# Query and key projections in Strassen blocks, in a stage of their own ahead of attention

## The chip, the core and the metric

The kernel runs on one core of a Trainium2 chip. The metric is the device time of one launch in microseconds (us), from the first to the last instruction with what lies around them; lower is better. Before the change it is 963.37 us, the median of 3 runs (961.13 to 970.48). The engines are TensorE (PE in the profile; PEld is its weight load), VectorE (DVE), ScalarE (ACT), GpSimd (POOL) and SyncE (SP), on whose queue every DMA is issued.

## The reference

A decoder block on 1024 rows of 1024 channels: an RMS norm, one wide input projection, two attention branches side by side (FoX with a forgetting bias, and differential attention with rotary embedding), SiLU gates, and a merge by sigmoid gates.

```python
h = rms_norm(x, g_pre[l], NORM_EPS)
proj = jnp.einsum('bsd,dn->bsn', h, w_in[l])
qa, ka, va, fa, za, qb, kb, vb, zb, gates = jnp.split(proj, SPLIT_POINTS, axis=-1)
log_f = jax.nn.log_sigmoid((fa + b_forget[l]).astype(jnp.float32)).transpose(0, 2, 1)
ya = fox_attention(split_heads(qa, FOX_HEADS), split_heads(ka, FOX_HEADS),
                   split_heads(va, FOX_HEADS), log_f)
ya = merge_heads(ya) * jax.nn.silu(za)
qd = apply_rope(qb.reshape(b, s, DIFF_HEADS, 2, DIFF_QK_DIM).transpose(0, 2, 3, 1, 4), cos, sin)
kd = apply_rope(kb.reshape(b, s, DIFF_HEADS, 2, DIFF_QK_DIM).transpose(0, 2, 3, 1, 4), cos, sin)
yb = diff_attention(qd, kd, split_heads(vb, DIFF_HEADS), lam)
yb = rms_norm(yb, g_subln[l], SUBLN_EPS) * (1.0 - lam_init)
yb = merge_heads(yb) * jax.nn.silu(zb)
gate_a, gate_b = jnp.split(jax.nn.sigmoid(gates), N_BRANCHES, axis=-1)
merged = (gate_a * jnp.einsum('bsw,wd->bsd', ya, w_branch[l, 0])
          + gate_b * jnp.einsum('bsw,wd->bsd', yb, w_branch[l, 1]))
x = x + rms_norm(jnp.einsum('bsd,de->bse', merged, w_out[l]), g_post[l], NORM_EPS)
```

## The kernel before, in words

Every product is made from operands split in a high part of fewer mantissa bits and a low part, the rest; a product is then three matmuls: high by high, high by low, low by high. The normed and transposed input `hT` stays on the chip as high and low parts in four blocks each (halves of the channels, `kh`, and of the rows, `sh`).

The work goes through five stages. **Values** (lines 99 to 218): `x_block` norms and transposes 128 rows, `load_wv` loads and splits the value weights for one of 8 channel blocks, and `v_block` makes the values of 128 rows and stores them to DRAM. **Attention** (lines 248 to 612): 8 units, four of the differential branch (diff, u 0 to 3) and then four of the forgetting branch (fox, u 4 to 7, two heads each). For each unit queries and keys are projected (`unit_proj`: two chunks of 512 rows for each, 24 matmuls a chunk, `project`), turned by `rope` in the diff units, and laid by `stack` in four tiles TA, TB, KA, KB. A row block of 128 queries goes through `s_row`: score matmuls (S), a DVE pass that scales, adds the bias or mask and takes the running minimum, the exponential on ACT, a reciprocal on DVE, scaling on POOL. Two row blocks make a group, for which `av` transposes the probabilities on PE (pt), splits them on ACT (ph) and DVE (pl), and multiplies by the values (yp). **Gates** (lines 614 to 810): the merge gates' projection, for one of 8 column blocks in the plain way (`gates_plain`) and for the other 7 by `wino`, which makes a 2 by 2 block product from 7 block products in place of 8 (Winograd's form of Strassen's scheme). Its left operands are sums of weight blocks (S, split into `a`), its right operands blocks of `hT` and four combinations of them, T4 to T7, which `h_combinations` makes at the start of this stage. **Branches** (to line 851), and the **output** product with the last norm, again by `wino`.

The order of the instructions on each engine is set when the program is built, by a scheduler that works from a model of each instruction's duration; each engine then takes its queue in that order. In the attention stage the loop over units lists, beside the groups of unit u, the four projection chunks of unit u+1 and the two chunks of one z projection (`ZFILL`) as fillers between groups; the fillers are PE work that waits for no attention step. Buffers are set by pools: 6 tiles for probabilities (`pp`), 3 score banks (`sps`), 2 banks for transposes.

## Time and profile before

| | |
|---|---|
| runs | 963.37 us median of 3 (961.13 to 970.48) |
| the profiled execution's own time | 964.18 us, span 962.4 us |
| mean granted TensorE clock | 0.981 |
| busy, share of the span | PE 94%, DVE 66%, ACT 45%, POOL 51% |
| values | 0 to 111 us |
| attention with its projections | 111 to 598 us |
| gates | 598 to 773 us |
| branches and output | 773 to 962.4 us |

A row of the profile reads: line, engine, operation, what is written <- what is read, partitions x elements and type, times executed, busy us and mean ns of one, and then the idle time of the engine just before such an instruction, with what ended it. A matmul's recorded duration reaches to the modelled end of its pipeline, so that neighbours overlap; how fast PE goes is read from the count in a stretch. The stage limits in the table are read from the first and last start of pv, pk, pz, pg, x_g and pb matmuls.

### The profile page before, as it was taken

How to read it: one execution, taken by the hardware profiler on the slowest of the kernel's cores; microseconds unless marked ns; L12 is line 12 of the kernel's file. 1: busy time of each engine (PE TensorE's matmuls, PEld its weight loads, DVE VectorE, ACT ScalarE, POOL GpSimd, SP SyncE). 2: the span in 40 equal slices, each digit the busy share in tenths (PEclk: the TensorE clock that was granted, in tenths of full speed). 3: DMA queues.
4: the chain of work that ended last, by engine and by line, in shares of the span. 5: the costliest groups of instructions: out<-in, count | busy, mean ns of one | idle time of the engine just before them, and what ended most of it. 6: DMA issues, size and time to landing. Idle time of an engine off the chain costs nothing.

```text
span 962.4 us, 13682 instructions
## 1 busy us (share of the span) xinstructions
PE 900.5 (94%) x4600; PEld 752.0 (78%) x4600; DVE 635.3 (66%) x1180; ACT 435.9 (45%) x862; POOL 489.6 (51%) x460
## 2 busy tenths in 40 slices
PE   7999989999999999999999998879999989999992
PEld 5999867777887888888888886658887768887871
DVE  7731258978768765656566477985667683559875
ACT  3421125665656674555555566243444361324331
POOL 7100035446545464344533554935566735878972
PEclk9999989999999999999999999989999999999997
DMA  9532444424334341524225231254444697210144
GB/s 315 190 110 93 144 128 112 107 77 120 97 96 137 99 144 43 150 67 130 81 88 146 85 88 56 78 179 149 143 153 134 191 357 247 67 44 1 46 151 153
DMA packets 109896, 120.17 MB, mean 125 GB/s; under 512 B 9969, under 2 KB 79601, under 8 KB 109826
## 3 DMA queue, kind: packets, MB, share of 16 engines
q1 hardware_dynamic: 109826, 119.30, 40.0%
q8 instruction: 36, 0.59, 0.3%
q14 instruction: 34, 0.28, 0.1%
HBM read 77.26 MB, written 29.43 MB: 111 GB/s over the span
## 4 chain that ended last, share of the span: by engine, by line
PE 45%; DVE 17%; POOL 13%; issue 10%; DMA 7%; ACT 6%; SPq 2%; DVEq 0%; POOLq 0%; ACTq 0%
PE pb L835 9%; PE pv L192 9%; PE pz L243 7%; PE pq L243 5%; PE pk L243 4%; POOL S_g L646 3%; PE ypf L444 3%; PE ptf L420 2%; DMA raw<-in_w_in_dram 2%; DMA swk<-rawk 2%; SPq L284 2%; DVE Pd L393 1%; POOL a_g L634 1%; PE ypd L444 1%; PE Sf L391 1%
## 5 line engine op out<-in xcount | busy, mean ns | idle before, releaser
L192 PE MATMUL pv<-wvhi,hT 128*128 128x264 f32 (+2 forms) x384 | 88.8, 323 | 0.4 <-DVE hT L178 0.4
L682 PE MATMUL x_g<-T,a_g 128*128 128x512 f32 x336 | 82.1, 399 | 6.3 <-DVE a_g L634 2.5
L243 PE MATMUL pk<-hT,hi_k 128*128 128x512 f32 x256 | 84.5, 402 | 1.7 <-ACT rawk L280 1.7
L243 PE MATMUL pz<-hT,hi_z 128*128 128x512 f32 x256 | 84.2, 399 | 0.1
L243 PE MATMUL pq<-hT,hi_q 128*128 128x512 f32 x256 | 83.4, 399 | 0.0
L682 PEld LDWEIGHTS x_g<-T,a_g 128*128 128x128 f32 x336 | 63.4, 191 | 23.5 <-DVE a_g L634 4.0
L835 PE MATMUL pb<-yT,hi_br 128*128 128x512 f32 x256 | 78.9, 390 | 1.9 <-ACT hi_br L229 1.6
L682 PE MATMUL x_o<-wo_op,a_o 128*128 128x512 f32 x336 | 77.4, 391 | 2.3 <-ACT a_o L633 1.2
L682 PEld LDWEIGHTS x_o<-wo_op,a_o 128*128 128x128 f32 x336 | 62.8, 188 | 16.9 <-ACT a_o L633 2.1
L192 PEld LDWEIGHTS pv<-wvhi,hT 128*128 128x128 f32 x384 | 64.3, 189 | 6.1 <-DVE hT L178 0.7
L682 PE MATMUL x_g<-hT,a_g 128*128 128x512 f32 x252 | 62.2, 400 | 6.1 <-DVE a_g L634 5.4
L398 ACT ACTIVATE Pd<-Pd,mxd 128x128 f32<-128x128 f32 (+7 forms) x64 | 49.5, 773 | 29.9 <-DVE mxd L393 28.1
L512 POOL TENSOR_SCALAR Pf<-Pf,lf 128x1024 f32<-128x1024 f32 (+3 forms) x64 | 47.9, 752 | 29.0 <-DVE lf L400 27.2
L424 DVE TENSOR_TENSOR plf<-ptf,phf 128x512 fp32r<-128x512 f32 (+1 forms) x80 | 50.0, 635 | 18.8 <-ACT phf L423 17.8
L192 PE MATMUL pv<-wvlo,hT 128*128 128x512 f32 (+2 forms) x192 | 61.8, 324 | 0.6 <-DVE wvlo L148 0.6
L682 PEld LDWEIGHTS x_g<-hT,a_g 128*128 128x128 f32 x252 | 48.4, 193 | 17.6 <-DVE a_g L634 5.8
L482 POOL TENSOR_SCALAR Pd<-Pd,ld 128x128 f32<-128x128 f32 (+7 forms) x32 | 25.5, 798 | 71.1 <-DVE ld L481 38.2
L508 POOL TENSOR_TENSOR cb<-cb,trim 128x128 f32<-128x128 f32 x64 | 29.5, 464 | 63.3 <-DVE mxf L393 46.7
L398 ACT ACTIVATE Pf<-Pf,mxf 128x1024 f32<-128x1024 f32 (+3 forms) x64 | 49.7, 778 | 21.4 <-DVE mxf L393 20.8
L835 PEld LDWEIGHTS pb<-yT,hi_br 128*128 128x128 f32 x256 | 47.8, 188 | 12.7 <-ACT hi_br L229 2.0
L243 PEld LDWEIGHTS pk<-hT,hi_k 128*128 128x128 f32 x256 | 48.0, 192 | 11.2 <-issue 2.1
L243 PEld LDWEIGHTS pq<-hT,hi_q 128*128 128x128 f32 x256 | 48.0, 191 | 9.1
(243 smaller groups left out, 2440.5 us busy)
## 6 DMA issues: line engine op xcount, KB each, us to landing
raw<-in_w_in_dram SPq DMA_DIRECT2D x14, 512.0 KB, 4.0
g_d<-c_g SPq DMA_DIRECT2D x21, 256.0 KB, 2.0
vb_d<-vbs SPq DMA_DIRECT2D x8, 512.0 KB, 5.9
va_d<-vas SPq DMA_DIRECT2D x8, 512.0 KB, 3.0
raw_k<-in_w_in_dram SPq DMA_DIRECT2D x8, 512.0 KB, 4.3
raw_q<-in_w_in_dram SPq DMA_DIRECT2D x8, 512.0 KB, 4.4
V<-vb_d SPq DMA_DIRECT2D x4, 1024.0 KB, 7.4
raw_z<-in_w_in_dram SPq DMA_DIRECT2D x8, 512.0 KB, 5.4
```

The lines of the kernel that those rows point to most:

```text
L192: nc.tensor.matmul(ps[n], lhsT=hT[hp][k // 4][i // 4][:, k % 4, hs], rhs=wt[k][:, a:b], start=first, stop=(k == KT - 1 and hp == 1))
L243: nc.tensor.matmul(ps, lhsT=a[:, k, :], rhs=hT[h][k // 4][c][:, k % 4, :], start=(k == 0 and a is hi and h == 0), stop=(k == KT - 1 and a ...
L284: nc.sync.dma_start(sw[b * 32:(b + 1) * 32, :], raw[o * 32:(o + 1) * 32, :])
L398: nc.scalar.activation(pr[:, 0:n], pr[:, 0:n], AF.Exp, bias=mx[:, len(pcs) - 1:len(pcs)], scale=-1.0, accum_out=le)
L424: nc.vector.tensor_tensor(pl[:, 0:n], pt[:, 0:n], ph[:, 0:n], op=ALU.subtract)
L444: nc.tensor.matmul(o, lhsT=a, rhs=b[:, src], start=(j == 0 and n == 0), stop=(odd == 1 and jj == g and n == len(prods) - 1))
L482: nc.gpsimd.tensor_scalar(p2[:, 0:n], p2[:, 0:n], l2, 1.0, op0=ALU.mult, op1=ALU.mult)
L508: nc.gpsimd.tensor_tensor(diag, diag, trim, op=ALU.add)
L512: nc.gpsimd.tensor_scalar(p1[:, 0:n], p1[:, 0:n], l1, 1.0, op0=ALU.mult, op1=ALU.mult)
L646: eng.tensor_tensor(comb[name], x, y, op=op)
L682: nc.tensor.matmul(x[m], lhsT=a[:, ai, k, :], rhs=right[m][bi][k], start=(k == 0 and n == 0), stop=(k == 3 and n == 2))
L835: nc.tensor.matmul(ps, lhsT=a[:, kk, :], rhs=yT[g][h][:, k % 2, sl], start=(k == 0 and a is hi and h == 0), stop=(k == 3 and a is lo))
```

## The change

The projections of queries and keys leave the attention loop. Between values and attention stands a new stage: for each of the 8 units the query weights and the key weights are the upper and lower block rows of a left operand, and `wino` makes the queries and keys of both halves of the rows with 7 block products of 12 matmuls. `qk_out` turns the result in the diff units (in place, with the same four small DMAs that exchange halves), splits it into high and low part, and stores both to DRAM (`qk_d`). The units are taken in the order 0, 4, 1, 5, 2, 6, 3, 7. In the attention stage `unit_qk` loads the four tiles with 8 DMAs of 256 KB; `unit_proj`, `rope` and `stack` are gone. The fillers there are the z projections alone, one for each unit (`ZFILL`).

The combinations T4 to T7 are made in the values stage, 16 POOL additions, 16 DVE subtractions, 16 ACT copies and 16 DVE low parts as before, and serve the new stage; they are also stored to DRAM (`t_d`, 8 tiles of 1 MB) and loaded again at the start of the gates. The value weights are loaded and split in two groups, all 8 channel blocks of the diff values and then all 8 of the fox values and the forget column, the second in the first's tiles; all 8 row blocks of the first group come before those of the second.

```diff
-ZFILL = ((0,), (1,), (), (2,), (3,), (4,), (5,), (6, 7))
+ZFILL = ((0,), (1,), (2,), (3,), (4,), (5,), (6,), (7,))
+PAIRS = (0, 4, 1, 5, 2, 6, 3, 7)
+ORD = (1, 6, 5, 7, 2, 3, 4)
...
+    qk_d = [[[dram.tile([P, S], F32, name=f"qk_d{u}_{n}_{part}") for part in range(2)]
+             for n in range(2)] for u in range(8)]
...
+        def load_wv(k, grp):
+            c0, n = ((VB, 512), (VA, 520))[grp]
+            raw = xp.tile([P, 520], F32, tag="wvraw", name=f"wvraw{k}_{grp}", bufs=3)[:, 0:n]
+            nc.sync.dma_start(raw, w[k * P:(k + 1) * P, c0:c0 + n])
+            hi = wv_hi[grp][k] = vw.tile([P, 520], F32R, tag=f"wvhi{k}", name=f"wvhi{k}_{grp}")
+            lo = wv_lo[grp][k] = vw.tile([P, 520], F32R, tag=f"wvlo{k}", name=f"wvlo{k}_{grp}")
...
         for i in range(NB):
             if i + 3 < NB:
                 x_block(i + 3)
-            v_block(i)
+            v_block(i, 0)
+        for k in range(KT):
+            load_wv(k, 1)
+        for i in range(NB):
+            if i < 4:
+                h_combinations(i)
+            v_block(i, 1)
+        for m, ts in t_tiles.items():
+            for part in range(2):
+                nc.sync.dma_start(t_d[m][part], f32(ts[part]))
...
+        def qk_out(u, n, c, t):
+            sl = slice(c * CH, (c + 1) * CH)
+            nm = f"{u}_{n}_{c}"
+            if u < 4:
+                sw = rp.tile([P, CH], F32, tag="sw", name=f"sw{nm}")
+                for b in range(4):
+                    o = b ^ 1
+                    nc.sync.dma_start(sw[b * 32:(b + 1) * 32, :], t[o * 32:(o + 1) * 32, :])
+                nc.vector.tensor_tensor(t, t, cosT[:, sl], op=ALU.mult)
+                nc.gpsimd.tensor_tensor(sw, sw, sinT[:, sl], op=ALU.mult)
+                nc.vector.tensor_tensor(t, t, sw, op=ALU.add)
+            hi = rp.tile([P, CH], F32R, tag="qh", name=f"qh{nm}")
+            lo = rp.tile([P, CH], F32R, tag="ql", name=f"ql{nm}")
+            nc.scalar.copy(hi, t)
+            nc.vector.tensor_tensor(lo, t, hi, op=ALU.subtract)
+            for part, p in enumerate((hi, lo)):
+                nc.sync.dma_start(qk_d[u][n][part][:, sl], f32(p))
+
+        for u in PAIRS:
+            c0 = (QB, KB_) if u < 4 else (QA, KA_)
+            raw = []
+            for n in range(2):
+                r = wpool.tile([P, KT, P], F32, tag="wraw", name=f"rawqk{u}_{n}")
+                nc.sync.dma_start(r, w_cols(c0[n] + u % 4 * P))
+                raw.append(r)
+            left = left_operands(f"p{u}", raw[0][:, 0:4], raw[0][:, 4:8], raw[1][:, 0:4], raw[1][:, 4:8])
+            run_all(wino(f"p{u}", left, h_ops, ORD,
+                         *(lambda t, u=u, n=n, c=c: qk_out(u, n, c, t)
+                           for n in range(2) for c in range(2))))
...
-        def unit_proj(u):
...
+        def unit_qk(u):
+
+            T = {}
+            for m, h in enumerate("AB"):
+                for n, nm in enumerate("KT"):
+                    t = T[nm + h] = qk.tile([P, S], F32R, tag=nm + h, name=f"{nm}{h}{u}")
+                    for part, rows in enumerate((UPR, DNR)):
+                        nc.sync.dma_start(
+                            f32(t[rows]), qk_d[u][1 - n][part][m * 64:(m + 1) * 64])
+            return T
...
-    h_combinations()
+    for m in (6, 5, 7, 4):
+        ts = [tpool.tile([P, 4, CH], F32R, tag=f"T{m}{part}", name=f"U{m}{part}")
+              for part in range(2)]
+        for part in range(2):
+            nc.sync.dma_start(f32(ts[part]), t_d[m][part])
+        h_ops[m] = [[t[:, k, :] for k in range(4)] for t in ts]
     gates_plain(0)
```

How the order moves is shown at two places. The first is VectorE in the values stage, and before the change the start of the gates. Before, after the last attention step (`ys` is the sum of a fox group's two halves), the combinations stand one behind the other: `f` are the full blocks that are subtracted in place, `T` the low parts of the combinations.

```order
L776 TENSOR_TENSOR f_0_6759<-f_0_6757,f_0_6759 128x512
L780 TENSOR_TENSOR f_0_6757<-f_0_6761,f_0_6757 128x512
L773 TENSOR_TENSOR T_6750<-f_0_6759,T_6749 128x512
L773 TENSOR_TENSOR T_6754<-f_0_6757,T_6753 128x512
L778 TENSOR_TENSOR f_0_6759<-f_0_6761,f_0_6759 128x512
L782 TENSOR_TENSOR f_0_6763<-f_0_6763,f_0_6759 128x512
L776 TENSOR_TENSOR f_1_6779<-f_1_6777,f_1_6779 128x512
```

After the change the same steps stand in the values stage where the second group of weights comes in: `wvlo_1` are the low parts of that group's weights, for which PE waits, and `vas` is the first evacuation of a result of that group.

```order
L278 TENSOR_TENSOR wvlo_1_704<-wvraw_1_701,wvhi_1_703 128x520
L363 TENSOR_TENSOR f_1_807<-f_1_807,f_1_806 128x512
L278 TENSOR_TENSOR wvlo_1_710<-wvraw_1_707,wvhi_1_709 128x520
L353 TENSOR_TENSOR T_179<-f_1_806,T_178 128x512
...
L278 TENSOR_TENSOR wvlo_1_722<-wvraw_1_719,wvhi_1_721 128x520
L357 TENSOR_TENSOR f_2_881<-f_2_881 128x512
L361 TENSOR_TENSOR f_2_881<-f_2_882,f_2_881 128x512
L353 TENSOR_TENSOR T_177<-f_2_881,T_176 128x512
L278 TENSOR_TENSOR wvlo_1_728<-wvraw_1_725,wvhi_1_727 128x520
L359 TENSOR_TENSOR f_2_881<-f_2_882,f_2_881 128x512
L353 TENSOR_TENSOR T_181<-f_2_881,T_180 128x512
L337 TENSOR_TENSOR vas_799<-pv_10_749,vas_799 128x4x64
```

The weights' low parts, the evacuation and the combinations now share VectorE's queue; from the first combination to this evacuation it holds 12 of the 16 steps `f`, 10 of the 16 steps `T` and all 8 steps `wvlo_1`.

The second place is TensorE inside a fox unit, between the last groups of one unit and the first of the next. Before, projection chunks of the unit after (`pk`, `pq`) stand between the attention steps.

```order
L243 MATMUL pk_1_5521<-hT_91,hi_k_5364 128x512
L243 MATMUL pk_1_5521<-hT_95,hi_k_5364 128x512
L444 MATMUL ypf_0_1_5171<-phf_0_1_0_5173,V_4550 128x256
L444 MATMUL ypf_0_1_5171<-plf_0_1_0_5174,V_4550 128x256
...
L420 MATMUL ptf_1_1_1_5240<-ident,Pf_1_2_5161 128x128
...
L391 MATMUL Sf_0_6_0_5333<-KA_4558,TA_4556 128x512
L392 MATMUL Sf_0_6_0_5333<-KA_4558,X0f_3_5313 128x512
L243 MATMUL pk_1_5521<-hT_91,lo_k_5365 128x512
...
L243 MATMUL pq_1_5550<-hT_89,hi_q_5399 128x512
```

After the change attention steps stand there alone.

```order
L527 MATMUL Sf_1_6_0_5451<-KB_5306,X1f_3_5431 128x512
L579 MATMUL ypf_0_0_5283<-phf_0_0_0_5285,V_4634 128x256
L579 MATMUL ypf_0_0_5283<-plf_0_0_0_5286,V_4634 128x256
...
L526 MATMUL Sf_1_6_1_5455<-KB_5306,TB_5309 128x384
...
L526 MATMUL Sf_0_5_0_5537<-KA_5300,TA_5303 128x512
...
L526 MATMUL Sf_0_4_1_5556<-KA_5300,TA_5303 128x256
L527 MATMUL Sf_0_4_1_5556<-KA_5300,X0f_2_5532 128x256
L555 MATMUL ptf_0_3_0_5464<-ident,Pf_0_6_5337 128x128
```

The fillers that are left, the z chunks, are not spread evenly either: the scheduler puts the z projections 0 to 3 into unit 0, one into the start of each of units 2, 3 and 4, the last into the middle of unit 4, and none into units 1, 5, 6 and 7.

397 lines of the change are left out of this document (179 added, 218 removed).

## The prediction

> **What bounds the kernel now.** I read the head of the page first, then the shares of the chain that ended last, then busy time by stage, then the groups.
>
> ```profile
> span 962.4 us, 13682 instructions
> PE 900.5 (94%) x4600; PEld 752.0 (78%) x4600; DVE 635.3 (66%) x1180; ACT 435.9 (45%) x862; POOL 489.6 (51%) x460
> PE 45%; DVE 17%; POOL 13%; issue 10%; DMA 7%; ACT 6%; SPq 2%; DVEq 0%; POOLq 0%; ACTq 0%
> ```
>
> TensorE is busy for 94% of the span, yet it holds only 45% of the chain, and DVE and POOL hold 30%. So PE's work bounds the kernel in some stretches and the handing on between the engines in others. The windows (start:end, length, busy us and instructions of PE, PEld, DVE, ACT, POOL, then granted PE clock, DMA share, GB/s) show which.
>
> ```profile
> 0.00:111.00 111.00, 104.30 (x646) 91.98 (x647) 48.31 (x80) 29.95 (x61) 26.72 (x48) 1.00 0.49 171
> 111.00:598.00 487.00, 468.41 (x2552) 395.67 (x2550) 333.67 (x834) 277.08 (x586) 225.42 (x250) 0.99 0.36 102
> 165.00:185.00 20.00, 17.87 (x84) 14.51 (x83) 19.64 (x37) 10.18 (x21) 10.40 (x8) 0.91 0.45 112
> 565.00:598.00 33.00, 29.30 (x201) 24.58 (x199) 25.92 (x80) 26.07 (x60) 17.80 (x29) 1.00 0.15 45
> 598.00:640.00 42.00, 33.32 (x127) 26.00 (x127) 38.19 (x32) 13.95 (x25) 32.27 (x21) 0.88 0.27 88
> 640.00:773.00 133.00, 128.75 (x558) 103.67 (x557) 88.25 (x105) 55.94 (x96) 79.70 (x54) 1.00 0.54 172
> 680.00:700.00 20.00, 20.00 (x90) 16.56 (x89) 11.90 (x16) 7.83 (x15) 11.39 (x9) 1.00 0.52 158
> 773.00:962.00 189.00, 165.72 (x723) 134.64 (x721) 126.88 (x131) 59.00 (x98) 125.48 (x89) 0.97 0.39 131
> ```
>
> Values (first row) and the later gates (640 to 773) are PE's. At 680 to 700, 90 matmuls of 128x512 fill 20 us: **0.222 us each**, the price used below (0.433 ns a column). The start of the gates (598 to 640) is DVE's: 38.2 of 42 us busy, and PE has only 127 matmuls, 28 us of work. Attention is mixed: at 165 to 185 DVE is busy 98% of the time, while over the whole stage it is 69%.
>
> **Arithmetic.** Queries and keys take 8 x 4 chunks x 24 = 768 matmuls before and 8 x 7 x 12 = 672 after. 96 x 0.222 = 21.3 us is all that PE saves. What decides is how well each new stage is filled.
>
> **Attention without its fillers.** What a unit asks of PE and of DVE comes from these rows (fox first, then diff; each covers 4 units).
>
> ```profile
> 567.62 1.04 PE L420 MATMUL ptf<-ident,Pf 128*128 128x128 f32 x8
> 568.41 0.36 PE L391 MATMUL Sf<-KA,TA 128*128 128x256 f32 x1
> L420 PE MATMUL ptf<-ident,Pf 128*128 128x128 f32 x288 | 44.2, 275 | 2.0 <-DVE plf L424 1.9
> L444 PE MATMUL ypf<-phf,V 128*128 128x256 f32 (+1 forms) x160 | 42.2, 285 | 1.0 <-DVE ys L522 0.4 <-ACT phf L423 0.3
> L391 PE MATMUL Sf<-KA,TA 128*128 128x512 f32 (+3 forms) x48 | 17.5, 366 | 0.6 <-DVE mxf L393 0.6
> L243 PE MATMUL pz<-hT,lo_z x128: 387/389/628, 172.1 to 565.7; 128*128 128x512 f32 x128
> L424 DVE TENSOR_TENSOR plf<-ptf,phf 128x512 fp32r<-128x512 f32 (+1 forms) x80 | 50.0, 635 | 18.8 <-ACT phf L423 17.8
> L393 DVE CUSTOM_DVE_ANT_0 Pf<-Sf,cb 128x512 f32<-128x512 f32 (+1 forms) x64 | 36.4, 569 | 22.0 <-PE ptf L420 15.6 <-PE Sf L392 4.7 <-POOL cb L508 0.9
> L393 DVE CUSTOM_DVE_ANT_0 Pf<-Sf,cb,mxf 128x256 f32<-128x256 f32 (+2 forms) x32 | 18.6, 580 | 5.2 <-PE Sf L392 3.9 <-POOL cb L508 0.7 <-POOL Pf L512 0.2
> L522 DVE TENSOR_TENSOR ys<-ypf,yt 64x256 f32<-64x256 f32 x32 | 13.4, 418 | 20.5 <-ACT yt L521 19.9
> L400 DVE RECIPROCAL lf<-lf 128x1 f32<-128x1 f32 x64 | 10.2, 161 | 14.5 <-ACT Pf L398 14.4
> L424 DVE TENSOR_TENSOR pld<-ptd,phd 128x512 fp32r<-128x512 f32 (+1 forms) x40 | 24.9, 632 | 6.9 <-ACT phd L423 6.7
> L393 DVE CUSTOM_DVE_ANT_0 Pd<-Sd,dmask 128x512 f32<-128x512 f32 (+3 forms) x64 | 35.9, 567 | 8.1 <-POOL Pd L485 3.9 <-PE Sd L392 3.8
> L393 DVE CUSTOM_DVE_ANT_0 Pd<-Sd,dmask,mxd 128x256 f32<-128x256 f32 (+2 forms) x32 | 18.5, 577 | 0.5
> L400 DVE RECIPROCAL ld<-ld 128x1 f32<-128x1 f32 x64 | 9.9, 158 | 12.0 <-ACT Pd L398 11.4
> L481 DVE TENSOR_TENSOR ld<-ld,nlam 128x1 f32<-128x1 f32 x32 | 9.8, 306 | 0.6
> ```
>
> A burst of 8 transposes and the next matmul start 0.79 us apart (567.62, 568.41): 0.099 us each. A fox unit has 36,864 columns of scores and values (16.0 us) and 288/4 = 72 transposes (7.1): PE 23.1 us. A diff unit has 32,256 columns (14.0) and 36 transposes (3.6): PE 17.6. DVE needs (50.0 + 36.4 + 18.6 + 13.4 + 10.2)/4 = **32.2 us** in a fox unit and (24.9 + 35.9 + 18.5 + 9.9 + 9.8)/4 = **24.8** in a diff unit. Without fillers DVE is the longer engine in both; before, the projections lie under it.
>
> How full DVE can be then, the last fox unit shows. After the last z matmul (565.7) there is no filler, and the window 565 to 598 does 201 - 5 = 196 of the 72 + 48 + 80 = 200 matmuls of a fox unit, and 25.9 of its 32.2 us of DVE. By the matmuls a fill-free fox unit takes 33.7 us, by DVE's work 41; it is the stage's end, with nothing behind it, so I take the middle, **37 us** (ends 33 at DVE's 98% of the window 165 to 185, and 41). A fill-free diff unit at 25.9/33 = 0.8 of DVE is 30, and 3 more for starting on loaded tiles.
>
> z is 384 matmuls, 10.7 us each of eight. Their places are known: four in unit 0, one each in units 2 and 3, two in unit 4. Where PE has fill, its whole share of before holds: 1152 x 0.222 + 4 x (17.6 + 23.1) = 418.5 of 487, 0.86; unmixed projection work runs at 558 x 0.222 / 133 = 0.93. Unit 0: (42.6 + 17.6)/0.93 = 65. Unit 1: 33. Units 2 and 3: 28.3/0.86 = 33 each. Unit 4: (23.1 + 21.3)/0.86 = 52. Units 5 to 7: 3 x 37 = 111. Sum **327 us** (290 to 350).
>
> **Values.** PE's work stays, but DVE and POOL get the combinations.
>
> ```profile
> L773 DVE TENSOR_TENSOR T<-f,T 128x512 fp32r<-128x512 f32 x16 | 18.9, 1203 | 1.5 <-ACT T L772 1.5
> L776 DVE TENSOR_TENSOR f<-f,f 128x512 f32<-128x512 f32 x4 | 6.0, 1496 | 1.8 <-POOL f L767 1.8
> L782 DVE TENSOR_TENSOR f<-f,f 128x512 f32<-128x512 f32 x4 | 4.7, 1175 | 0.1
> L767 POOL TENSOR_TENSOR f<-hT,hT 128x512 f32<-128x512 f32 x16 | 25.8, 1645 | 5.5 <-PE ypf L444 3.6 <-DVE T L773 1.8
> L148 DVE TENSOR_TENSOR wvlo<-wvraw,wvhi 128x512 fp32r<-128x512 f32 (+1 forms) x16 | 12.6, 818 | 0.8 <-POOL wvhi L146 0.8
> L675 DVE TENSOR_TENSOR cu_g<-x_g,cu_g 128x512 f32<-128x512 f32 x14 | 9.5, 682 | 0.4
> ```
>
> In VectorE's queue 12 subtractions, 10 low parts and 8 `wvlo_1` stand ahead of the first evacuation of the second group: 12 x 1.34 + 10 x 1.20 + 8 x 0.82 = 34.6, about 36 us with the three other steps there. PE has meanwhile two blocks of the first group and, with two banks' rows to fill, two of the second: (48 + 48 x 520/512) x 0.222 = 21.5 us. It waits 36 - 21.5 = **14 us**, and values take 125. The price of these steps is the question: with both inputs beside POOL's additions they take 1.2 to 1.5 us, a step of the same size that reads a matmul's result takes 0.68 (L675). At 0.68 the queue is 22 us and the cost +1. The upper end, if all 16 + 16 steps came first, is +22.
>
> The Trainium skill, "SBUF — State Buffer", section "Who interferes with whom", gives a reason: a DVE instruction with two SBUF inputs shares a read port with GpSimd's reads, and whichever comes second waits for the whole instruction. By that rule the dear price moves along with POOL's additions, as the rows have it, and the +1 would be out of reach.
>
> **The new stage.** Its price is that of `wino` in the gates, and of the rope.
>
> ```profile
> L634 DVE TENSOR_TENSOR a_g<-S_g,a_g 128x512 fp32r<-128x512 f32 x28 | 30.1, 1075 | 24.5 <-ACT a_g L633 24.5
> L285 DVE TENSOR_TENSOR rawk<-rawk,cosT 128x512 f32<-128x512 f32 x8 | 6.5, 807 | 15.5 <-DMA swk<-rawk 15.5
> L287 DVE TENSOR_TENSOR rawk<-rawk,swk 128x512 f32<-128x512 f32 x8 | 8.8, 1098 | 1.3 <-POOL swk L286 1.2
> ```
>
> PE: 84 matmuls a unit, 18.6 us, 149 in all; at the gates' 0.93 that is 160. DVE in a fox unit: 5 splits x 1.08, 7 additions x 0.68, 4 low parts x 1.08 = 14.5. In a diff unit 4 x (0.81 + 1.10) = 7.6 more, and some 3 us of waiting for the exchange of halves (before 15.5 us over 8 keys' chunks): 25, more than PE's 18.6. Diff and fox units alternate, so DVE's mean is 19.8, 158 in all. With 5 us of start and drain **164 us** (155 to 180). The upper end is that the two don't even out: 4 x 25 + 4 x 18.6 + 6.
>
> **Gates.** The T steps go; the 96 plain matmuls stay, 684 in all, at the pace of 640 to 773 (133/558 = 0.238): **163 us**, 12 less than 598 to 773. T comes back as 8 MB.
>
> ```profile
> V<-vb_d SPq DMA_DIRECT2D x4, 1024.0 KB, 7.4
> wo<-in_w_out_dram SPq DMA_DIRECT2D x4, 1024.0 KB, 10.7
> ```
>
> A tile of 1 MB lands 7.4 to 10.7 us after its issue. The plain gates cover 21 us and the first of the seven products needs no T. I cost the reload at nothing; were the eight to land one by one at 7.4, the last would come some 60 us in, and with the seven products paced by it that costs up to 10. Storing q, k and T (24 MB, and 16 MB read back) falls where the windows show DMA shares of 0.15 to 0.5: nothing.
>
> **Sum.** 125 + 164 + 327 + 163 + 189.4 (773 to 962.4 is untouched) = 968.4. Around the span lie 1.8 us (964.18 against 962.4), giving 970; the profiled execution is 0.8 above the median of the runs, so **969 us**.
>
> **The rivals.**
>
> *B, attention keeps DVE full.* For it: the 98% of 165 to 185, and that no buffer is then held for projections. Against: the last unit's 0.8. Unit 1 takes 27, units 2 and 3 30, unit 4 48, units 5 to 7 33 each, unit 0 62: 296, total 938. It decides for faster once attention is below 311.
>
> *D, the combinations hide in values.* The cheap price holds, 13 us less: 956. For it: DVE is busy 48 of 111 us there. Against: the 38.2 of 42 us at the same steps in the gates.
>
> *E, the slower side: the new stage runs at DVE's pace* in the diff units because PE cannot run ahead into the fox unit (its left operands stand behind the rope on DVE). 180 in place of 164: 985. It decides for slower from 168 on. For it: the 15.5 us at L285. Against: the alternating order.
>
> *C, the clock.* Where PE is starved its granted clock falls: 0.88 in the DVE-bound stretch 598 to 640. If it fell to half in units 1 and 5 to 7, PE's 23.1 becomes 46 and exceeds DVE: 3 x 9 + 2 = 29 more, 998. Against: 1.00 in the fill-free window 565 to 598. The Trainium skill, "TensorE: Matmul & The Clock Gate", section "HAM oscillation — how this bites in real kernels", has the clock halve when PE idles over some 3.4 us at a stretch; the gaps of a fill-free unit are under 1 us by the rows' idle times, so by that rule C would not come.
>
> That the matmuls are not saved is out: 672 are in the order.
>
> **How the numbers follow.** A measurement of this kernel tells about 1% (9.6 us) from no change: 953.7 to 973.0. Main case 0.42 (own range 955 to 983), B 0.17, D 0.15, E 0.18, C 0.08. Faster: B, 0.06 of D, 0.04 of the main case: 0.27. Same: 0.22 of the main case, 0.09 of D, 0.02 of E: 0.33. Slower: the other 0.16, 0.16 of E, C: 0.40. The range leaves out C and B's lower half: 941 to 993.
>
> **What would show it.** In the changed kernel's windows: values 125 us with PE idle at the first `vas` on DVE; the new stage 164 with 672 matmuls, and idle before `x_p` put to DVE; fox units 5 to 7 about 37 us each with DVE near 87% and a clock near 1.00; gates 163 with no wait for a T load. Attention under 311 or above 345, or a new stage over 175, makes the prediction wrong.

## The result and the profile after

The changed kernel takes 1025.83 us (median of 4 runs, 1024.9 to 1026.89) where the kernel before takes 963.68: a ratio of 1.064, 95% interval 1.059 to 1.069. The forecast was 969 us, with a range of 941 to 993. The profiled execution after the change took 1026.89 us, with a span of 1025.1.

The head of the page, its chain by engine, and the stages in windows (start:end, length, busy us and instructions of PE, PEld, DVE, ACT, POOL, then PE clock, DMA share, GB/s). The stages are bounded by the first starts of `x_p`, `pz`, `pg` and `pb` matmuls.

```profile
span 1025.1 us, 13931 instructions
PE 913.9 (89%) x4504; PEld 749.5 (73%) x4504; DVE 668.2 (65%) x1228; ACT 444.0 (43%) x878; POOL 536.9 (52%) x492
PE 39%; DMA 18%; DVE 15%; POOL 10%; issue 8%; ACT 6%; SPq 2%; DVEq 0%; POOLq 0%; ACTq 0%
```

```profile
0.00:129.70 129.70, 110.75 (x644) 95.49 (x644) 78.50 (x114) 40.64 (x78) 48.35 (x61) 0.95 0.57 199
129.70:319.30 189.60, 161.75 (x673) 129.71 (x673) 144.15 (x160) 53.91 (x95) 103.09 (x68) 0.95 0.54 163
319.30:670.20 350.90, 314.26 (x1785) 258.46 (x1785) 227.68 (x722) 230.50 (x507) 176.74 (x218) 0.95 0.58 154
670.20:834.20 164.00, 159.61 (x685) 130.50 (x686) 92.63 (x103) 62.12 (x106) 87.68 (x59) 0.98 0.62 210
834.20:1025.10 190.90, 167.51 (x721) 135.33 (x719) 125.25 (x131) 56.88 (x96) 121.07 (x88) 0.95 0.40 132
```

The 96 matmuls are saved: 4504 against 4600. TensorE is busy for a smaller share of a longer span (89% against 94%), and transfers now hold 18% of the chain in place of 7%. Yet its busy time has grown, to 913.9 us from 900.5: its mean granted clock is 0.954, before 0.981, so that many matmuls take longer. By stage:

| stage | before | forecast | after | missed by |
|---|---|---|---|---|
| values | 111 | 125 | 129.7 | +4.7 |
| new stage for q and k | | 164 | 189.6 | +25.6 |
| attention | 487 | 327 | 350.9 | +23.9 |
| gates | 175 | 163 | 164.0 | +1.0 |
| branches and output | 189.4 | 189.4 | 190.9 | +1.5 |

In attention 487 - 350.9 = 136 us came free; the new stage costs 189.6. That is 53.5 us of the loss. Values and gates together add 18.7 - 11.0 = 7.7, branches and output 1.5. Two terms of the sum were wrong, each by about 25 us, and the experiments are about these two.

In the new stage PE stops at the start of every diff unit but the first, and runs through the four fox units without a stop. By the starts of their first matmuls the diff units after the first take 25.2, 25.6 and 25.6 us in place of 19, and two fox units 22.7 and 21.6, as the diff unit after them begins late. The timeline round the third diff unit, one row of each queue in order of time: ACT, then SyncE (SPq), PE, POOL, and PE again.

```profile
201.41 0.62 ACT L410 CAST qh<-c_p 128x512 fp32r<-128x512 f32 x1 [7.55 <-DVE c_p L407]
210.08 0.51 SPq L404 DMA_DIRECT2D sw<-cu_p  x1
210.63 0.59 SPq L420 DMA_DIRECT2D rawqk<-in_w_in_dram  x1
215.78 4.85 PE L204 MATMUL x_p<-hT,a_p 128*128 128x512 f32 x12 [3.46 <-ACT a_p L153]
216.81 1.28 POOL L167 TENSOR_TENSOR S_p<-rawqk 128x512 f32<-128x512 f32 x1 [2.90 <-DMA rawqk<-in_w_in_dram]
223.74 9.60 PE L204 MATMUL x_p<-T,a_p 128*128 128x512 f32 x34 [2.48 <-DVE a_p L154]
241.34 2.88 PE L204 MATMUL x_p<-hT,a_p 128*128 128x512 f32 x12
```

```profile
210.00:230.00 20.00, 14.06 (x45) 9.94 (x44) 16.97 (x21) 7.75 (x14) 9.65 (x6) 0.83 0.69 217
```

ACT stands 7.55 us at the copy `qh` of a rotated result. The next weights (`rawqk`) are issued directly behind the last exchange of halves (`sw`), and PE waits for the left operands `a_p` made from them. The window 210 to 230 holds 45 matmuls where 90 fit, so some 10 us are lost there. At the end of the stage PE idles once more, until VectorE's last addition of a result of this stage (`cu_p`). This wait is called the drain below.

```profile
319.29 0.77 PE L139 MATMUL pz<-hT,hi_z 128*128 128x512 f32 x1 [11.57 <-DVE cu_p L197]
```

The rotation's steps and the low parts behind it on DVE, and its product on POOL, by groups:

```profile
L411 DVE TENSOR_TENSOR ql<-c_p,qh 128x512 fp32r<-128x512 f32 x24 | 29.9, 1245 | 4.3 <-ACT qh L410 2.2 <-DMA qk_d<-ql 2.0
L405 DVE TENSOR_TENSOR c_p<-c_p,cosT 128x512 f32<-128x512 f32 x12 | 14.1, 1176 | 7.0 <-DMA sw<-c_p 6.1 <-issue 0.9
L407 DVE TENSOR_TENSOR c_p<-c_p,sw 128x512 f32<-128x512 f32 x12 | 16.0, 1329 | 1.4 <-POOL sw L406 1.2
L406 POOL TENSOR_TENSOR sw<-sw,sinT 128x512 f32<-128x512 f32 x16 | 26.5, 1659 | 30.6 <-DMA sw<-c_p 16.6 <-DMA sw<-cu_p 11.4 <-DVE c_p L407 2.6
```

In attention the units are bounded by the last `y_d` store of each diff unit: unit 0 takes 88.5 us (forecast 65), unit 1 38.9. Windows of unit 0, unit 1 and the rest:

```profile
319.30:407.80 88.50, 77.90 (x369) 64.58 (x369) 42.07 (x132) 40.69 (x91) 26.07 (x27) 0.88 0.78 204
407.80:446.70 38.90, 35.67 (x204) 29.11 (x205) 26.68 (x92) 29.87 (x68) 25.87 (x25) 1.00 0.63 165
446.70:670.20 223.50, 200.70 (x1213) 164.76 (x1211) 158.94 (x499) 159.94 (x351) 124.80 (x167) 0.97 0.49 133
```

The chain of waits inside unit 0 shows what it waited for: loads of q and k, and behind them the weights of a z projection (`raw_z`), which took 10 us where 6.6 is the median.

```profile
346.44 5.61 DMA KB<-qk_d
352.11 10.07 DMA raw_z<-in_w_in_dram
362.26 1.05 POOL hi_z L127
```

### The profile page after: what moved, and what is told of

It reads as the page before. It is cut to its first block, busy times and chain, and to the rows that moved or that the text cites. A ratio compares the mean times of both kernels' runs of the same rounds, so it can differ in the third digit from the quotient of the medians.

```text
span 1025.1 us, 13931 instructions
## 1 busy us (share of the span) xinstructions
PE 913.9 (89%) x4504; PEld 749.5 (73%) x4504; DVE 668.2 (65%) x1228; ACT 444.0 (43%) x878; POOL 536.9 (52%) x492
## 4 chain that ended last, share of the span: by engine, by line
PE 39%; DMA 18%; DVE 15%; POOL 10%; issue 8%; ACT 6%; SPq 2%; DVEq 0%; POOLq 0%; ACTq 0%
PE x_g L204 10%; PE pz L139 6%; PE pb L854 5%; PE pv L321 5%; DMA rawqk<-in_w_in_dram 3%; PE ypf L579 2%; PE pg L139 2%; PE ptf L555 2%; DMA cb<-cum_d 2%; DMA y_d<-ys 2%; POOL S_p L167 2%; DMA va_d<-vas 1%; DMA raw_z<-in_w_in_dram 1%; DMA sw<-c_p 1%; DVE ql L411 1%
## 5 line engine op out<-in xcount | busy, mean ns | idle before, releaser
L204 PE MATMUL x_p<-T,a_p 128*128 128x512 f32 x384 | 95.7, 406 | 10.4 <-DVE a_p L154 7.5
L139 PE MATMUL pz<-hT,hi_z 128*128 128x512 f32 x256 | 85.8, 409 | 14.6 <-DVE cu_p L197 11.6
L321 PE MATMUL pv<-wvhi,hT 128*128 128x256 f32 (+2 forms) x384 | 94.1, 334 | 5.2 <-POOL wvhi L277 3.4
L204 PEld LDWEIGHTS x_p<-T,a_p 128*128 128x128 f32 x384 | 75.0, 197 | 29.2 <-DVE a_p L154 8.8
L204 PE MATMUL x_g<-U,a_g 128*128 128x512 f32 x336 | 80.5, 396 | 2.9 <-ACT a_g L153 2.5
L204 PEld LDWEIGHTS x_g<-U,a_g 128*128 128x128 f32 x336 | 64.0, 191 | 17.5 <-ACT a_g L153 3.3
L204 PE MATMUL x_p<-hT,a_p 128*128 128x512 f32 x288 | 70.3, 398 | 6.9 <-ACT a_p L153 5.8
L321 PE MATMUL pv<-wvlo,hT 128*128 128x256 f32 (+2 forms) x192 | 64.2, 337 | 6.3 <-DVE wvlo L278 6.3
L204 PEld LDWEIGHTS x_p<-hT,a_p 128*128 128x128 f32 x288 | 54.6, 191 | 20.0 <-ACT a_p L153 6.7
L139 PEld LDWEIGHTS pz<-hT,hi_z 128*128 128x128 f32 x256 | 50.1, 198 | 25.6 <-issue 12.0
L643 POOL TENSOR_TENSOR cb<-cb,trim 128x128 f32<-128x128 f32 x64 | 29.3, 460 | 71.1 <-DVE mxf L528 39.3
L154 DVE TENSOR_TENSOR a_g<-S_g,a_g 128x512 fp32r<-128x512 f32 x28 | 30.3, 1084 | 43.6 <-ACT a_g L153 43.6
L854 PEld LDWEIGHTS pb<-yT,hi_br 128*128 128x128 f32 x256 | 48.5, 190 | 12.3 <-DVE yT L844 1.6
```

What stands on the lines that cost most here:

```text
L139: nc.tensor.matmul(ps, lhsT=a[:, k, :], rhs=hT[h][k // 4][c][:, k % 4, :], start=(k == 0 and a is hi and h == 0), stop=(k == KT - 1 and a ...
L154: eng.tensor_tensor(lo, src, hi, op=ALU.subtract)
L204: nc.tensor.matmul(x[m], lhsT=a[:, ai, k, :], rhs=right[m][bi][k], start=(k == 0 and n == 0), stop=(k == 3 and n == 2))
L321: nc.tensor.matmul(ps[n], lhsT=hT[hp][k // 4][i // 4][:, k % 4, hs], rhs=wt[grp][k][:, a:b], start=first, stop=(k == KT - 1 and hp == 1))
L643: nc.gpsimd.tensor_tensor(diag, diag, trim, op=ALU.add)
L854: nc.tensor.matmul(ps, lhsT=a[:, kk, :], rhs=yT[g][h][:, k % 2, sl], start=(k == 0 and a is hi and h == 0), stop=(k == 3 and a is lo))
```

## The experiments

Each is one profiled execution, beside the kernel before on the same chip (961.6 to 963.6 us); the last has five timed rounds more. "The stage" is the new stage from its first `x_p` to the first z matmul, 189.6 us in the changed kernel by that rule; the expectations give it as 188.5. In the five attention experiments that keep the stage and have z it took 188.3 to 189.3, so 1 us in it tells nothing and 3 us stand out.

### The new stage

**The rotation left out.**

```diff
-            if u < 4:
+            if False:
                 sw = rp.tile([P, CH], F32, tag="sw", name=f"sw{nm}")
```

> The changed kernel with the rotation of the diff units left out in the new stage: no exchange of halves, no multiplications by cos and sin, no addition (queries and keys of the diff units come out unrotated). The new stage took 188.5 us (129.5 to 318) against 164 forecast. Theory 1, the rotation holds up the next unit's left operands (its exchanges stand before the next weights in SyncE's queue, its copies before the next splits on ACT): the stage falls to about 160 us, total about 1000. Theory 2, DVE's work as such: DVE loses 35 us of its 143 in the stage, and the stage falls by up to that, 153 to 165, the same total; this run prices the rotation and the next one tells the theories apart. Theory 3, the two weight buffers or the outputs' stores, whatever the rotation: the stage stays above 180, total above 1015.

Measured: 991.08 us, the stage 157.2. Its window:

```profile
131.30:288.50 157.20, 153.17 (x672) 125.92 (x673) 92.58 (x128) 53.93 (x95) 71.71 (x52) 1.00 0.56 169
```

TensorE waits for no left operand any more and runs at its full clock (1.00 against 0.95). The rotation costs 32.4 us of stage, and theory 3 falls: with the stores and the two weight buffers as they are the stage comes near the 149 us of its matmuls. The 32.4 us have three parts. PE's waits for left operands are 16.2 us (8.7 put to ACT, 7.5 to DVE), with the rotation left out none. The drain falls from 11.6 us to 3.9. And the same 672 matmuls are busy for 161.8 us with the rotation and 153.2 without it, at the lower clock.

**The weights on another queue.**

```diff
-                nc.sync.dma_start(r, w_cols(c0[n] + u % 4 * P))
+                nc.gpsimd.dma_start(r, w_cols(c0[n] + u % 4 * P))
```

> The weight loads of the new stage are issued from GpSimd's queue in place of SyncE's; nothing else. In the trace the weights of the third diff unit were issued at 210.6 us behind exchanges that wait for the rotation, 5 us after the last use of their buffer (205.4). Theory 1 (SyncE's order holds the weights back): each of three diff units gains about 5 us, the stage falls from 188.5 to 173 to 178, total about 1012. Theory 2 (DVE's work) and the form of theory 1 in which only ACT's order counts: no change, 1020 to 1030.

Measured: 1032.06 us, the stage 194.1. POOL's queue in the same place:

```profile
204.49 0.93 POOL L420 DMA_DIRECT2D rawqk<-in_w_in_dram  x1 [0.30 <-POOL a_p L154]
208.75 0.93 POOL L420 DMA_DIRECT2D rawqk<-in_w_in_dram  x1 [0.30 <-POOL a_p L154]
215.19 1.69 POOL L406 TENSOR_TENSOR sw<-sw,sinT 128x512 f32<-128x512 f32 x1 [5.51 <-DMA qk_d<-qh]
216.84 1.73 POOL L167 TENSOR_TENSOR S_p<-rawqk 128x512 f32<-128x512 f32 x1
```

The weights are issued 2 to 6 us earlier, as theory 1 has it, and nothing is gained: the sum `S_p` begins at 216.84, before at 216.81, since it now stands behind a product of the rotation. The wait taken from one in-order queue came back in the next.

**The rotation without its exchange.**

```diff
-                for b in range(4):
-                    o = b ^ 1
-                    nc.sync.dma_start(sw[b * 32:(b + 1) * 32, :], t[o * 32:(o + 1) * 32, :])
-                nc.vector.tensor_tensor(t, t, cosT[:, sl], op=ALU.mult)
-                nc.gpsimd.tensor_tensor(sw, sw, sinT[:, sl], op=ALU.mult)
+                nc.gpsimd.tensor_tensor(sw, t, sinT[:, sl], op=ALU.mult)
+                nc.vector.tensor_tensor(t, t, cosT[:, sl], op=ALU.mult)
```

> The rotation keeps its arithmetic (two steps on DVE and one on POOL for each result of a diff unit), but without the exchange of halves through DMA: the products with sin are made from the unexchanged result (so diff queries and keys are not those of the reference). Without the rotation the new stage took 157 us, with it 188.5; moving the weights to GpSimd's queue gained nothing, since the next unit's sums then began at the same time (216.84 against 216.81 us) behind a product with sin that waited for its exchange. Theory 1 in this form (each in-order queue in turn is held by the exchange's round trip): the stage falls to 157 to 168, total 993 to 1007. Theory 2 (the rotation's work on DVE and POOL, beside each other at 1.2 to 1.7 us a step): the stage stays at 180 to 188, total 1015 to 1028.

Measured: 1024.98 us, the stage 186.5. Taking the exchange out gains 3 us; this form of theory 1 falls. But PE no longer waits in the same place. The diff units after the first now take 21.6, 21.2 and 19.3 us, and the three fox units after them 25.6, 26.6 and 25.3: PE stops inside each of these fox units for a left operand of that unit, whose copy on ACT and low part on DVE stand behind rotated results.

```profile
209.93 3.62 PE L204 MATMUL x_p<-hT,a_p 128*128 128x512 f32 x10 [3.65 <-DVE a_p L154]
```

**The exchange without the arithmetic**, its counterpart: the steps with cos and sin go, `t = sw`.

> The exchange of halves stays, the arithmetic of the rotation is left out (the exchanged halves are split and stored as they are): 2 steps fewer on DVE and one on POOL for each of 16 results, 35.6 us of DVE and 26.5 of POOL in the changed kernel. Theory A: the exchange still holds the queues, the stage stays at 175 to 186, total 1010 to 1022. Theory B: the stage falls to 157 to 168, total 992 to 1004.

Measured: 1016.19 us, the stage 176.8. Its window:

```profile
129.50:306.30 176.80, 158.83 (x672) 128.31 (x673) 103.90 (x128) 54.47 (x95) 73.49 (x52) 0.97 0.58 174
```

That is within theory A and far from theory B. So the exchange alone costs 176.8 - 157.2 = 19.6 us, the arithmetic alone 186.5 - 157.2 = 29.3, and both together 32.4, not 49: each hides most of the other.

**The last split of the weights earlier.** Left operand 4 is the last use of the weight buffers.

```diff
+            def left2(m, left=left, early=early):
+                if m == 2:
+                    early[4] = left(4)
+                return early[4] if m == 4 else left(m)
```

> The changed kernel; in the new stage the split of the last raw weight block (left operand 4) is listed before left operand 2, so that it stands ahead of the copies of the rotated results in ACT's queue, and the weight buffers come free sooner. Theory 1b (both weight buffers hold the current unit; their last use waits on ACT behind copies that wait for the rotation; the next unit's weights, sums and splits then come late, and PE idles 6 to 10 us in front of three units): the next weights are issued some 8 us earlier, the stage falls from 188.5 to 165 to 178, total 1002 to 1015. Theory 2 (DVE's and POOL's own time for the rotation): no change, 1020 to 1030.

Measured: 1016.85 us, the stage 181.3, 8.3 less: theory 1b is right in kind, below the size that it expected. PE still waits for `a_p`, 1 to 2.5 us at a time: no longer ahead of a unit, but inside two diff units and the three fox units after the first.

**The last two together.**

> The early split of operand 4 and the rotation without its exchange, both at once. Alone the first took the new stage from 188.5 to 181 us and the second to 186.5; without the whole rotation it was 157. Theory A (the exchange and the late weights hide each other: while one is left the next unit's operands are late): together the stage falls to 157 to 168, total 992 to 1004. Theory B (the rotation's arithmetic on DVE and POOL costs the rest, whatever waits): 175 to 181, total 1010 to 1018.

Here "the rotation without its exchange" is joined with the early split. Measured: 1015.15 us, the stage 177.2. Theory A, in which the two hide each other, falls; 177.2 is theory B's figure. But theory B fell with the exchange alone, so neither holds for the whole. All of PE's waits for `a_p` are now inside fox units.

**The steps behind the exchange listed later.**

```diff
-                nc.vector.tensor_tensor(t, t, cosT[:, sl], op=ALU.mult)
-                ...
+                late.append(lambda: qk_turn(u, n, c, t, sw))
```

> The exchange starts as now, but the steps after it (products with cos and sin, sum, split, store) are listed one at a time behind the products of the next unit. In ACT's queue two or three splits of the next unit's left operands move ahead of the copies that wait for the rotation. Theory 1: PE's idle time at the start of diff units 1 to 3 (6 to 10 us each) shrinks; the stage falls by 5 to 20 us, total 1005 to 1020. Theory 2: no change, 1021 to 1030.

Measured: 1026.11 us, the stage 185.7. A gain of 4 us there, lost again behind it; the total is that of theory 2, which expected no change. The run is inconclusive.

What stands: the rotation as a whole costs 32 us, by making left operands late, and either half of it, transfers or arithmetic, is enough for more than half of that. With the exchange in place the late operands are the next diff unit's; with the arithmetic alone they are mostly those of the fox unit that runs beside it. How the two share the cost in the changed kernel isn't settled. More weight buffers, the plain cure for the late loads, weren't tried.

### Attention

**Unit 0 without its loads.** Its four tiles are copied from `hT` by ACT.

```diff
+                    if u == 0:
+                        for c in range(2):
+                            nc.scalar.copy(t[:, c * CH:(c + 1) * CH], hT[0][0][c][:, 2 * m + n, :])
+                        continue
```

> The first attention unit takes its four q and k tiles from copies of the normed input on the chip, made by ACT, and not from DRAM (so this unit's scores are not those of the reference; all else is kept). Unit 0 took 90 us (318 to 408) against 65 forecast, and its first score matmul came 13.8 us after the last projection. Theory 4, the start waits for the round trip through DRAM: the first score comes within 4 us, unit 0 falls to 70 to 78, total 1010 to 1014. Theory 5, unit 0 is long because four z projections and cold pipelines lie in it: the first score comes earlier, but the unit still takes 85 to 92, total 1020 to 1030.

Measured: 1022.86 us. Unit 0 ends 77.8 us after the first z matmul (88.5 before), attention takes 344.4: 6.5 less. The total fell by 3 to 4 only, as values and what follows attention came out 1 to 2 us longer in this execution. Theory 4 is right on the unit (70 to 78), and not on the total or on the first score, which comes 7.8 us after the first z matmul (12.5 in the changed kernel) and not within 4.

**No loads of q and k at all.** Units 0 and 1 take copies, later units the tiles of two units before.

> No q and k tile is loaded from DRAM in attention: units 0 and 1 take them from copies of the normed input, later units use the tiles of the unit two before (so scores are not those of the reference); the stores stay. Without the loads of unit 0 alone attention fell by 7 us (352 to 345). Theory 4 (only the first round trip counts, later loads are hidden): attention again about 345, total 1016 to 1023. Theory 6 (14 MB more of loads slow the other transfers in attention): attention below 338, total below 1012.

Measured: 1006.05 us. Attention, unit 0, and units 2 to 7:

```profile
318.20:649.00 330.80, 305.48 (x1784) 252.42 (x1784) 227.74 (x722) 236.97 (x519) 176.26 (x218) 0.98 0.38 113
318.20:396.20 78.00, 73.23 (x369) 61.59 (x369) 42.97 (x134) 47.24 (x105) 26.89 (x28) 0.95 0.51 152
434.40:649.00 214.60, 197.08 (x1215) 161.10 (x1215) 161.28 (x504) 160.82 (x352) 126.47 (x169) 0.99 0.33 99
```

Attention is 20.1 us shorter, and theory 6 holds. With the reload gone it takes 331 us, the forecast's 327 but for 4. Of the 20.1 us, 8.8 are again PE's busy time on the same matmuls (314.3 against 305.5).

**The loads kept, their bytes gone.** From unit 2 on each load stands where it stood and brings 32 columns.

```diff
+                    cols = slice(0, S if u < 2 else 32)
                     for part, rows in enumerate((UPR, DNR)):
                         nc.sync.dma_start(
-                            f32(t[rows]), qk_d[u][1 - n][part][m * 64:(m + 1) * 64])
+                            f32(t[rows, cols]), qk_d[u][1 - n][part][m * 64:(m + 1) * 64, cols])
```

> Units 0 and 1 load q and k from DRAM as in the changed kernel; from unit 2 on each of the 8 loads stays at its place in SyncE's queue with its wait for the unit two before, but brings 32 columns of 1024 into the old tile (so scores are not those of the reference): 64 KB a unit in place of 2 MB. Without any of these loads attention took 331 us, with all 352, without unit 0's 345. Theory 6a (the bytes of the reload slow the other transfers): 337 to 344. Theory 6b (the loads' places and waits in SyncE's in-order queue cost): 349 to 354. Theory 6c (units 0 and 1 alone cost it, in the stretch 318 to 360 with DMA engines busy 90% and more): 349 to 354 too, with units 2 to 7 as long as in the changed kernel.

Measured: 1021.6 us, attention 346.3, of it units 2 to 7:

```profile
450.70:666.10 215.40, 195.56 (x1208) 159.86 (x1206) 155.09 (x494) 158.68 (x349) 124.63 (x167) 0.99 0.34 99
```

It lies between the figures, because unit 0, whose loads are kept, came out at 92.9 us, 4.4 more than in the changed kernel (PE waited 7.3 us for the high part of a z weight, there 3.0). In units 2 to 7 the bytes cost 223.5 - 215.4 = 8 us, and the loads' places in the queue under 1 (without the loads these units take 214.6). The other 11 of the 20 us are in units 0 and 1; in unit 0 DMA engines are at 0.78 over 88 us. So 6a holds in part (units 2 to 7), 6c in part (units 0 and 1 cost more than half), and 6b falls.

**z spread.** The weights of each z wait for a result of the unit before.

```diff
+        if after is not None:
+            nc.sync.dma_start(raw[0:1, 0, 0:32], after)
```

> The weights of each z projection but the first wait for a result of the unit before, by a small load from that result into the same tile ahead of them; so one z projection lies in each unit, and unit 0 has only one. Theory 5 (the fillers' place costs: PE is short of work in units 1, 5, 6 and 7 and overfull in 0): 3 x 10.7 = 32 us of z leave unit 0 for units bound by DVE, and attention falls from 352 by 15 to 30 us, total 995 to 1010. Theory 4 (round trip): z covers the start and is missed there, attention changes by under 8 us, 1017 to 1033.

Measured: 1047.15 us, 21 us slower; attention 373.7. Unit 0 falls to 78.7, but two fox units with z take 50 and 54 us. The last stores of fox units 4, 5 and 6:

```profile
555.11 0.33 SPq L665 DMA_DIRECT2D y_d<-ys  x1
605.25 0.32 SPq L665 DMA_DIRECT2D y_d<-ys  x1
659.69 0.34 SPq L665 DMA_DIRECT2D y_d<-ys  x1
```

Theory 5 is wrong on the sign, and theory 4 on the size. Two fox units that took 34 and 38 us without z grow by 16 us each, more than the 10.7 us of z. Part of the loss is the edit's own: since the weights of z are held back, PE waits for their high parts in five places (once, for 3.0 us, in the changed kernel), 3.6 and 3.3 us of it in these two units.

```profile
PE pz L142 <- POOL hi_z L130: 14.4, 5, 3.6
```

Even without these waits the two units would be 12.5 to 13 us longer, so the runs show no free time for z there. What z spread over the units would cost with its weights in time was not run.

**z in smaller pieces**, four of 6 matmuls for each chunk, listed between the score rows.

> As the run that spread z over all units, but each z chunk is listed in four pieces of 6 matmuls between the score rows; in the order of the fox units z then stands in runs of 19 to 22 matmuls in place of 44. The spread kernel took 1047 us, its fox units 5 and 6 50 and 54 us against 34 and 38 without z. Theory 7 (a run of 44 matmuls holds up the chain of attention steps for 10 us): units 5 and 6 fall by about 5 us each, total 1030 to 1040. Theory 8 (z adds its PE time to a fox unit however it is cut): 1044 to 1050.

Measured: 1044.94 us, attention 371.7, units 5 and 6 45.6 and 56.9 us. Unit 5 gains 4.5 us and unit 6 loses 2.5; the total is theory 8's. Shorter runs of z are no cure; the weights are held back here in the same way (PE waits 12.3 us for their high parts).

**No z.** A part of `hT` is stored in its place.

> The z projections are left out of attention (a part of the input is stored in their place), nothing else: 384 matmuls, 85 us of PE at 0.222 us. Attention took 352 us with them, of them 90 in unit 0 and 34 to 39 in the units without z. Theory 5a (attention steps keep their own pace, set by DVE and the chain between the engines, and z adds to it almost whole): attention falls to 270 to 290 us, total 943 to 963. Theory 5b (z lies under the steps of DVE): attention falls by less than 40 us, total above 985.

Measured: 998.12 us, attention 321 us (from 320, where z used to begin, to the first gates' matmul). Its first score begins at 332.7, after a wait of 22.5 us that the profile puts to `nlam`; 12.7 us of this wait lie in the window, the rest in the drain before it. In the changed kernel the first score comes just as late, 12.5 us after the first z matmul, but z covers the wait. The window, and that row of its waits:

```profile
320.00:641.20 321.20, 246.87 (x1400) 200.21 (x1400) 220.74 (x717) 227.52 (x506) 163.70 (x210) 0.86 0.58 158
```

```profile
PE Sd L522 <- DVE nlam L682: 22.5, 1, 22.5
```

This is theory 5b, with that wait in it. With TensorE busy for 247 of 321 us its granted clock is 0.86 over the window. What z costs lies between 30 us and 30 + 13 of its 85.

### Values and gates

**This part alone**: the values in two groups with the T combinations, T stored and reloaded; q and k projected in attention as before.

> One part of the change alone: values in two groups, the T combinations made there, stored and loaded again at the gates; queries and keys projected inside attention as before the change. By the two traces values grew by 18.5 us (111 to 129.5) and gates shrank by 11 (175 to 164), so the sum is +7: 969 to 972 with the kernel before at 961.6 on this chip. If the stores of T or the reload disturb attention or the gates beyond that: above 975. If the forecast's +14 and -12 hold: 964 to 966.

Measured: 970.6 us. Values 129.0, attention 486.2, gates 163.6:

```profile
0.00:129.00 129.00, 110.08 (x648) 94.72 (x648) 79.66 (x111) 39.44 (x76) 51.32 (x64) 0.96 0.59 209
129.00:615.20 486.20, 465.05 (x2552) 392.70 (x2550) 331.50 (x836) 277.20 (x586) 226.90 (x250) 0.99 0.37 104
615.20:778.80 163.60, 156.79 (x685) 127.92 (x685) 95.11 (x105) 63.09 (x106) 85.88 (x59) 1.00 0.63 217
```

7 us slower than before, as the stages said: the combinations cost the values 18 us where their going saves the gates 11, and storing and reloading T disturbs neither attention (486.2 against 487) nor the gates.

**The combinations where DVE has room.** The kernel before, with the four steps of `h_combinations` as fillers in units 4, 5 and 6, T stored and loaded at the gates.

```diff
+TFILL = ((), (), (), (), (0, 1), (2,), (3,), ())
...
+            for n, k in enumerate(TFILL[u]):
+                fill.insert(2 * n + 1, t_task(k))
```

> The kernel before the change with one idea of it: the T combinations are made in attention, where DVE and POOL have room beside the projections (units 4, 5 and 6: DVE at 55 to 63%), stored to DRAM and loaded at the gates. The part run alone in the values cost 18.5 us there and gained 11 to 12 in the gates. Theory 9 (PE bounds attention in these units and the 42 us of DVE work lie under it): attention 487 to 491 us, gates 164, total 950 to 956 with 962 before. Rival: the burst of steps holds up attention's own steps on DVE: attention grows by 10 to 20 us and the total is 961 to 972.

Measured: 955.13 us, and in five rounds:

> The kernel before with the T combinations made in attention, once more in five rounds, for the interval. By the one look (955.1 against 963.6): 0.988 to 0.994 of the kernel before.

952.99 us against 963.54: ratio 0.989, 95% interval 0.987 to 0.992. Attention and gates in this run:

```profile
111.00:598.20 487.20, 467.77 (x2552) 393.82 (x2550) 360.52 (x867) 285.82 (x602) 253.69 (x266) 0.99 0.41 120
598.20:761.80 163.60, 156.90 (x685) 127.93 (x685) 94.99 (x105) 63.10 (x106) 85.96 (x59) 1.00 0.64 217
```

DVE carries 27 us more in attention (360.5 against 333.7) in the same 487 us, and the gates keep the 11 us. Theory 9 holds. This version takes 1.1% less than the kernel before, a small gain, but its interval leaves out no change.

## Why the prediction was wrong

- **Arithmetic, right.** 96 matmuls fewer; worth 21 us only where PE sets the pace.
- **Gates 163, right** (164.0). The reload of T is hidden behind the plain gates, as costed.
- **Values 125, nearly** (129.7), but by other terms than those of the sum. It had 14 us of waiting at the first `vas`. PE does not wait there (its one wait for a `vas`, near the end of the stage, is 1.6 us); it stops at the second group's weights instead, 6.3 us for VectorE's low parts and 3.4 for POOL's high parts:

```profile
72.81 0.74 PE L321 MATMUL pv<-wvhi,hT 128*128 128x256 f32 x4 [2.49 <-POOL wvhi L277]
76.61 0.58 PE L321 MATMUL pv<-wvlo,hT 128*128 128x256 f32 x1 [3.05 <-DVE wvlo L278]
L353 DVE TENSOR_TENSOR T<-f,T 128x512 fp32r<-128x512 f32 x16 | 15.0, 940 | 0.7 <-ACT T L352 0.7
```

  A T low part took 0.94 us on the mean, between the two prices weighed (1.20 and 0.68), so the queue was shorter than said; POOL's high parts the sum left out. It also left out that matmuls slow down: the same products are busy for 110.8 us at a clock of 0.95, before 104.3 at 1.00. That the total came near is in part luck. The tile's row in the last section has 0.68 us as its shortest and 1.78 as its longest. The Trainium skill, "SBUF — State Buffer", section "Who interferes with whom", lets a step with two SBUF inputs wait out a whole GpSimd instruction; the trace agrees with it in the spread. That the mean hangs on how much POOL runs beside (32 of 42 us in the gates before, 48 of 130 in the values) fits, but was not tested apart. Rival D (combinations hidden) did not come.
- **New stage 164: the step that failed** is "Diff and fox units alternate, so DVE's mean is 19.8", with which the stage was priced by the busy time of two engines. DVE's work did not exceed PE's on the mean (144 of 189.6 us busy), but a diff unit's rotation is done while the next fox unit is computed, and the weights, sums and splits of the diff unit after that queue behind it. 84 matmuls need 18.6 us, but the third diff unit began at 215.8 us, 3.46 late, and the next unit at 241.3. The waits (16.2 us) and the slower matmuls (8.6 us) had no term, and the drain (11.57 us) was put at 5 with the start. Rival E had the size (180), and its 25 us for a diff unit is what three of the four took, but that is luck: it is not DVE's pace, since without the rotation's arithmetic, and with 40 us less on DVE (103.9 against 144.2), the stage still takes 177. E's left operands behind the rotation are there, but those of the next diff unit and not of the fox unit, in which PE stops only when the exchange is left out or the last split is moved.
- **Attention 327: the step that failed** is the last sentence on gates, "storing q, k and T ... falls where the windows show DMA shares of 0.15 to 0.5: nothing". The 16 MB read back cost 20 us. Those shares were of the kernel before; with the reload the share is 0.78 in unit 0, and there the z weights and the q and k tiles of two units wait for each other.
- **Inside attention two errors cancel, which is luck.** Without the reload the stage came to 331, but unit 0 still takes 78 us (forecast 65) and the last three fox units are shorter than the 37 us each: with the reload they take (670.2 - 572.0)/3 = 33. The stores that bound units 3 and 4:

```profile
520.50 0.53 SPq L628 DMA_DIRECT2D y_d<-ys  x1
571.97 0.33 SPq L660 DMA_DIRECT2D y_d<-ys  x1
```

  Why unit 0 takes 13 us more than its 60 us of PE work at 0.93 isn't settled; some 3 us of it, by their columns, are 22 score matmuls of unit 1 that stand in its window (70 where a unit has 48).
- **Rival B** (attention at 296) is refuted: 331 without any reload. **Rival C**, the clock, did not come where it was put: the granted clock is 1.00 in unit 1 and 0.97 in units 2 to 7. Elsewhere it came in part: 0.954 over the span (0.981 before), 0.88 in unit 0, and 0.86 where z is left out. That it is low where PE is starved is what the rows show. In busy time of the same matmuls (whose ends are modelled, so this is an estimate) it was worth 8.6 us in the new stage and 8.8 in attention, by the runs without rotation and without reload. The Trainium skill, "TensorE: Matmul & The Clock Gate", section "HAM oscillation — how this bites in real kernels", ties the halved clock to idle stretches over some 3.4 us. The trace agrees so far as a low clock stands where such waits are quoted above (11.57 us ahead of unit 0, at 0.88; 3.46 us in the window 210 to 230, at 0.83). But shorter stops are followed by slow matmuls too: in the second diff unit, behind stops of 1.45 and 2.53 us with two matmuls between them, 34 matmuls took 9.61 us, where 36 take 8.32 in the unit before.

## What to carry to other kernels

Work that lies under another stage's waits is not worth its own length there: 768 matmuls, 170 us of PE at 0.222, freed 136 us of attention (156 without the reload) and cost 190 us in a stage of their own, with an eighth of them saved. Without the rotation the kernel takes 34.8 us less, without the reload 19.8; if the two add (they were not run together), some 971 us are left, still more than the 963.7 before. Before moving work out, price its whole round trip (weights in, chain behind it, stores, reload) in the stage that it will stand in, and look for the last use that frees a buffer in an in-order queue behind a wait. To move work the other way, into a stage where the engine that it needs has room (DVE at 69% in attention before), paid at once: the T combinations cost nothing under the projections.

## What the runs showed of the hardware that was not expected

- Two costs of one chain overlap for the most part: exchange 19.6 us, arithmetic 29.3, both 32.4. Taking one out by itself tells little of its share, and moves the wait to another place.
- A stop of TensorE costs more than its length. In the new stage 16.2 us of waits and 7.6 us more of drain went with 8.6 us more of busy time for the same 672 matmuls (clock 0.95 against 1.00).
- A transfer of 512 KB of z weights takes 4.2 us (median) without the q and k loads, 6.6 with them, and 10.07 at the worst, with DMA engines at 0.94 in the stretch 340 to 360. The small exchanges of queries (64 KB) go from 2.1 to 4.0 us. First without the loads, then with them, and the stretch.

```profile
raw_z<-in_w_in_dram SPq DMA_DIRECT2D x8, 512.0 KB, 4.2
raw_z<-in_w_in_dram SPq DMA_DIRECT2D x8, 512.0 KB, 6.6
X0d<-TA SPq DMA_DIRECT2D x32, 64.0 KB, 4.0
340.00:360.00 20.00, 20.00 (x103) 16.88 (x101) 7.15 (x31) 8.47 (x24) 5.64 (x8) 1.00 0.94 234
```

- Steps of one size and form on DVE differ by a factor of 2.6 (ns: shortest, median, longest). In the values a T low part took 0.94 us on the mean, at the gates 1.20.

```profile
L353 DVE TENSOR_TENSOR T<-f,T x16: 674/682/1775, 58.6 to 100.7; 128x512 fp32r<-128x512 f32 x16
```
